# The first weight transfers and the last output tile of a hybrid attention layer: smaller loads, a warm-up from a constant, a residual added on TensorE, sums of squares from PSUM, and three last pieces stored from two queues

## The chip, the cores and the metric

The kernel runs on one core of one Trainium2 chip. The metric is the device time of one execution in microseconds, lower is better. The kernel before takes 434.15 us, the median of 3 runs (433.91 to 434.34).

## What is computed

One decoder layer over 512 tokens of width 1024, in float32. One wide input projection feeds two token mixers (a sparse attention with compressed, selected and window branches, and a gated linear recurrence); each mixer's result is gated and projected to 1024 channels, the two are merged by sigmoid gates, one output projection follows, and the layer ends in a residual with layer norm. The change touches the first product of the input projection and the last lines:

```
h = x @ w_in + b_in                       # first product here: the columns f_b of w_in
...
y = sigmoid(gm_a) * (o_a @ w_branch_a) + sigmoid(gm_b) * (o_b @ w_branch_b)
out = layer_norm(alpha * x + y @ w_out, ln_g, ln_b)
# layer_norm(v) = (v - mean(v)) * rsqrt(mean((v - mean(v))^2) + 1e-5) * g + b
```

## The kernel before, in words

Every float32 product is made of three float32r products: an operand is split into a high part (a cast) and a low part (what the cast left over), and `hi*hi`, `hi*lo` and `lo*hi` are added up in PSUM. A split takes one cast and one subtraction, mostly the cast on ScalarE (ACT) and the subtraction on VectorE (DVE).

**The head (lines 154 to 200).** x comes transposed, in 8 blocks of 128 channels by 512 tokens; the weights of the first product, `w0`, come in 8 blocks of 128 by 512 (64 KB per 128 columns). Block 0 of each is loaded in two halves of 256 columns: x from the SyncE queue (`dma`), the weights from the ACT queue (`dma_act`, line 158). The blocks 1 to 7 follow on the SyncE queue, x and weights in turn. While they travel, seven small matmuls of zeros run on TensorE (line 165), from a tile that DVE fills by a memset (line 162). Then, for block 0, ACT casts the x halves (`h`, line 183), DVE casts the weight halves (`wh`, line 184) and makes the two low parts (`l`, line 185, and `wl`, line 186); 24 matmuls of 256 columns use them, in the order (x half, weight half) = (0,0), (1,0), (0,1), (1,1). Each further block is split whole (lines 193 to 196) and feeds 12 matmuls of 512 columns.

**The middle.** Some 40 column tiles of the input projection are multiplied one after the other, and a table of delays weaves the steps of the two mixers between their matmuls. The branch products and the gates follow. The change leaves all this as it is.

**The end (lines 904 to 947).** `wo` holds the split halves of `w_out`, with the mean over the output channels taken out, so that `y @ wo` has mean zero over the channels; `res[tt]` holds `alpha * x`, mean taken out likewise, for token tile `tt` of 128 tokens, in two halves of 512 channels. For each token tile and half 24 matmuls add up in one PSUM bank. When they end, DVE adds half of the sum to the residual (line 933), collects `bn_stats` (line 934) and multiplies by `ln_g` (line 936). After both halves, `bn_aggr` (938) gives the variance, ACT takes the root (941), DVE its reciprocal (942), and DVE scales each half and adds `ln_b` (946); each half is stored by a DMA on the SyncE queue. The last token tile is cut in three in its matmuls (512, 256, 256 channels), with the multiplication of the last piece put behind the aggregate (944), but it is scaled and stored in two halves:

```
    cuts = [(0, 0, 512), (1, 0, 256), (1, 256, 512)] if last else [(0, 0, 512), (1, 0, 512)]
    ...
    if last:
        V.tensor_tensor(xr[hf][:, a:b], xr[hf][:, a:b], lg[hf][:, a:b], ALU.mult)
    for hf in range(2):
        V.scalar_tensor_tensor(xr[hf], xr[hf], rs[:, 0:1], lbn[hf], ALU.mult, ALU.add)
        dma(out[c, 512 * hf:512 * hf + 512], xr[hf])
```

**What sets the order.** Matmuls, DMAs and the marked DVE lines stay in program order; a scheduler places the rest on their engines and puts in the waits between engines. Each engine works through its own queue in order. A DMA takes one of eight landing semaphores in turn, and waits until the DMA eight places before it, on whichever queue, has landed.

Of the kernel before, what the change touches and what calls it, by code (L numbers as in the profile page):

```python
# [17 lines left out]
DM = 1024  # L18
P = 128
# [79 lines left out]
def layer_kernel(ctx: ExitStack, tc: tile.TileContext, xT, xn, w0, wi, wf, wv, small, brow, consts,  # L99
# [55 lines left out]
    halves = slice(0, 256), slice(256, 512)  # L155
    for n in halves:
        dma(first[0][:, n], xT[:, 0, n])
        dma_act(first[1][:, n], w0[0][:, n])
    act_set("sigmoid_and_others")

    zero = T2(128)
    V.memset(zero, 0.0)  # L162
# [7 lines left out]
    for kt in range(KT):  # L170
# [9 lines left out]
        if kt == 0:  # L180

            for n in halves:
# [731 lines left out]
    for tt in range(4):  # L914
        c = slice(128 * tt, 128 * tt + 128)
        last = tt == 3
        cuts = [(0, 0, 512), (1, 0, 256), (1, 256, 512)] if last else [(0, 0, 512), (1, 0, 512)]
        bst = SM(6 * len(cuts), "bst")
        xr = res[tt]
        bank = (PT, PO, PA, PS)[tt]  # L920
        pso_ = [bank() for _ in cuts[:2]] + ([PT()] if last else [])
        seq = [(u, kt) for u in range(len(cuts)) for kt in range(8)]
        if tt == 0:
            seq = [(u, kt) for kt in range(8) for u in range(2)]
        for u, kt in seq:
            hf, a, b = cuts[u]
            hi, lo = wo[kt][hf]
            ps = pso_[u][:, 0:b - a]
# [3 lines left out]
            if kt == 7:  # L932
                V.scalar_tensor_tensor(xr[hf][:, a:b], ps, 0.5, xr[hf][:, a:b], ALU.mult, ALU.add)  # L933
                V.bn_stats(bst[:, 6 * u:6 * u + 6], xr[hf][:, a:b])  # L934
                if not (last and u == 2):
                    V.tensor_tensor(xr[hf][:, a:b], xr[hf][:, a:b], lg[hf][:, a:b], ALU.mult)
        ag = SM(2, "ag")
        V.bn_aggr(ag, bst[:, 0:6 * len(cuts)])  # L938
# [4 lines left out]
        if last:  # L943
            V.tensor_tensor(xr[hf][:, a:b], xr[hf][:, a:b], lg[hf][:, a:b], ALU.mult)
        for hf in range(2):
            V.scalar_tensor_tensor(xr[hf], xr[hf], rs[:, 0:1], lbn[hf], ALU.mult, ALU.add)  # L946
            dma(out[c, 512 * hf:512 * hf + 512], xr[hf])
# [81 lines left out]
```

## Time and profile before

| | before |
|---|---|
| median of 3 runs | 434.15 us (433.91 to 434.34) |
| the profiled execution's own time | 433.26 us |
| its span, first to last instruction | 431.4 us |
| mean granted TensorE clock | 0.996 |
| busy: PE / weight loads / DVE / ACT / POOL | 98% / 82% / 69% / 57% / 4% |
| DMA, mean over the span | 110 GB/s |

The profile is of one execution. Its own time is 1.86 us over its span; that part lies outside the instructions. PE is TensorE's matmuls, PEld its weight loads, SPq and ACTq are the queues from which DMAs are issued. Matmuls overlap in the records, so that the pace of a row of them is read from the chain of waits and not from the duration of one. Times in the rows below are from the span's start.

### The profile page before, as it was taken

How to read it: one execution, taken by the hardware profiler on the slowest of the kernel's cores; microseconds unless marked ns; L12 is line 12 of the kernel's file. 1: busy time of each engine (PE TensorE's matmuls, PEld its weight loads, DVE VectorE, ACT ScalarE, POOL GpSimd, SP SyncE). 2: the span in 40 equal slices, each digit the busy share in tenths (PEclk: the TensorE clock that was granted, in tenths of full speed). 3: DMA queues.
4: the chain of work that ended last, by engine and by line, in shares of the span. 5: the costliest groups of instructions: out<-in, count | busy, mean ns of one | idle time of the engine just before them, and what ended most of it. 6: DMA issues, size and time to landing. Idle time of an engine off the chain costs nothing.

```text
span 431.4 us, 6047 instructions
## 1 busy us (share of the span) xinstructions
PE 424.1 (98%) x2173; PEld 355.3 (82%) x2173; DVE 298.6 (69%) x610; ACT 244.6 (57%) x490; POOL 16.0 (4%) x26
## 2 busy tenths in 40 slices
PE   9999999999999999999999999999999999999994
PEld 8888888888898878878888888888888888888884
DVE  5925669987786477956765666678655797872674
ACT  3434624713548455668866667788865975538300
POOL 2000000000011320000000010001001100000000
PEclk9999999999999999999999999999999999999998
DMA  8996400352320654141112111111144651072031
GB/s 271 394 356 217 148 1 2 85 149 87 123 73 2 188 147 152 52 145 50 49 51 95 49 51 49 50 49 55 45 148 160 215 161 50 0 217 77 19 129 49
DMA packets 20878, 47.57 MB, mean 110 GB/s; under 512 B 2928, under 2 KB 4592, under 8 KB 20848
## 3 DMA queue, kind: packets, MB, share of 16 engines
q1 hardware_dynamic: 20560, 46.92, 33.0%
q8 instruction: 17, 0.28, 0.3%
q10 hardware_dynamic: 288, 0.26, 0.2%
q14 instruction: 13, 0.11, 0.1%
HBM read 41.93 MB, written 2.10 MB: 102 GB/s over the span
## 4 chain that ended last, share of the span: by engine, by line
PE 98%; DVE 1%; DVEq 0%; issue 0%; ACT 0%
PE pa L107 62%; PE pss L107 17%; PE pso L107 12%; PE pst L111 5%; PE pst L107 3%; DVE t L946 0%; DVEq L1025 0%; DVE sm_bst L934 0%; DVE t L933 0%; ACT sm_rs L941 0%; DVE sm_ag L938 0%; DVE sm_rs L942 0%; DVE t L162 0%
## 5 line engine op out<-in xcount | busy, mean ns | idle before, releaser
L107 PE MATMUL pa<-t,whi 128*128 128x512 f32 x640 | 201.9, 397 | 0.0
L107 PEld LDWEIGHTS pa<-t,whi 128*128 128x128 f32 x640 | 116.9, 188 | 25.1 <-issue 2.0
L107 PE MATMUL pa<-t,wlo 128*128 128x512 f32 x320 | 125.2, 391 | 0.0
L151 DVE TENSOR_TENSOR wlo<-wraw,whi 128x1024 fp32r<-128x1024 f32 x46 | 57.0, 1241 | 23.4 <-ACT whi L150 23.1
L107 PEld LDWEIGHTS pa<-t,wlo 128*128 128x128 f32 x320 | 60.1, 188 | 13.2
L150 ACT CAST whi<-wraw 128x1024 fp32r<-128x1024 f32 x46 | 48.2, 1048 | 36.4 <-PE pa L107 17.7
L647 DVE CUSTOM_DVE_ANT_0 t<-pss,t 128x512 f32<-128x512 f32 (+3 forms) x64 | 30.1, 488 | 22.7 <-PE pss L107 22.5
L650 ACT ACTIVATE t<-t,sm_mn 128x512 f32<-128x512 f32 (+3 forms) x64 | 35.8, 561 | 9.0 <-DVE sm_mn L647 6.9
L151 DVE TENSOR_TENSOR t<-pst,t 128x512 fp32r<-128x512 f32 x40 | 27.5, 690 | 15.8 <-ACT t L150 15.8
L107 PE MATMUL pa<-t,t 128*128 128x512 f32 (+1 forms) x168 | 36.7, 375 | 0.0
L107 PEld LDWEIGHTS pa<-t,t 128*128 128x128 f32 x168 | 30.3, 188 | 5.6
L107 PE MATMUL pss<-t,t 128*128 128x512 f32 (+3 forms) x222 | 34.5, 310 | 0.0
L150 ACT CAST t<-pst 128x512 fp32r<-128x512 f32 x40 | 23.2, 580 | 18.9 <-PE pst L111 18.8
L107 PE MATMUL pso<-t,t 128*128 128x512 f32 (+2 forms) x158 | 32.9, 343 | 0.0
L107 PEld LDWEIGHTS pss<-t,t 128*128 128x128 f32 (+1 forms) x222 | 27.5, 175 | 3.7 <-issue 0.7
L111 PE MATMUL pst<-con,t 128*128 128x128 f32 x189 | 28.6, 272 | 0.0
L107 PEld LDWEIGHTS pso<-t,t 128*128 128x128 f32 x158 | 25.3, 190 | 3.8
L111 PEld LDWEIGHTS pst<-con,t 128*128 128x128 f32 x189 | 23.2, 140 | 4.2 <-DVE t L151 0.2
L107 PE MATMUL pso<-t,vv 128*128 128x512 f32 x80 | 23.1, 410 | 0.0
L151 DVE TENSOR_TENSOR t<-t,t 128x512 fp32r<-128x512 f32 (+1 forms) x22 | 14.2, 665 | 10.9 <-ACT t L150 10.9
L150 ACT CAST t<-t 128x512 fp32r<-128x512 f32 (+1 forms) x22 | 12.7, 603 | 15.5 <-DVE t L895 14.8
L107 PE MATMUL pss<-t,whi 128*128 128x512 f32 x64 | 19.7, 389 | 0.0
(166 smaller groups left out, 532.5 us busy)
## 6 DMA issues: line engine op xcount, KB each, us to landing
wraw<-in_wf_dram SPq DMA_DIRECT2D x38, 512.0 KB, 3.6
wraw<-in_wbr_dram SPq DMA_DIRECT2D x8, 512.0 KB, 3.8
t<-in_wout_dram SPq DMA_DIRECT2D x16, 256.0 KB, 3.2
t<-in_w_dram SPq DMA_DIRECT2D x15, 256.0 KB, 5.1
t<-t SPq DMA_DIRECT2D x48, 64.0 KB, 2.0
t<-in_wi_dram SPq DMA_DIRECT2D x8, 256.0 KB, 6.0
t<-in_xn_dram SPq DMA_DIRECT2D x8, 256.0 KB, 6.1
out_dram<-t SPq DMA_DIRECT2D x8, 256.0 KB, 2.1
```

The source lines that it names most:

```text
L107: return tc.keep_in_program_order(nc.tensor.matmul(*a, **k))
L111: return tc.keep_in_program_order(nc.tensor.transpose(*a, **k))
L150: A.copy(dst_hi, src)
L151: V.tensor_tensor(dst_lo, src, dst_hi.bitcast(F32), ALU.subtract)
L647: V.tensor_tensor_reduce(out=p[:, c], in0=ps[:, c], in1=amask[:, 512 - n:512], op0=ALU.add, op1=ALU.min, scale=-0.125, scalar=3.0e38, accu ...
L650: A.activation(p[:, c], p[:, c], AF.Exp, bias=mn[:, k], scale=-1.0, accum_out=den[:, k])
```

## The change

In the head, block 0's weights are loaded in three transfers of 128, 128 and 256 columns in place of two of 256, and cast in those pieces; the zeros of the warm-up are a constant that POOL writes in the program's preamble, and the memset on DVE goes.

In the last token tile the three pieces are written out by themselves. The first two are added to their residual on DVE as before, but ACT sums their squares (`Square` with an accumulator) in place of `bn_stats`; the mean is zero, so the mean square is the variance. For the third piece, twice the residual is split in high and low part ahead of time (`r2h`, `r2l`), and two matmuls with an identity (`eye`) add it in PSUM, after the first three matmuls of the piece. ACT then squares that piece from PSUM, takes the root of the total with what it knows of the first two pieces as the bias, DVE multiplies the piece by `ln_g` from PSUM, takes the reciprocal, and scales three pieces (512, 256, 256 channels), stored from the SyncE, ACT and SyncE queues.

```diff
+    wcuts = slice(0, 128), slice(128, 256), slice(256, 512)
     for n in halves:
         dma(first[0][:, n], xT[:, 0, n])
+    for n in wcuts:
         dma_act(first[1][:, n], w0[0][:, n])
...
-    zero = T2(128)
-    V.memset(zero, 0.0)
+    zero = nc.const_aps.tensor(0.0, [P, 128], F32)
...
             for n in halves:
                 A.copy(h[:, n], xr[:, n])
-                tc.keep_in_program_order(V.tensor_copy(wh[:, n], wr[:, n]))
-                tc.keep_in_program_order(V.tensor_tensor(l[:, n], xr[:, n], h[:, n].bitcast(F32), ALU.subtract))
-                tc.keep_in_program_order(V.tensor_tensor(wl[:, n], wr[:, n], wh[:, n].bitcast(F32), ALU.subtract))
+            for n, cuts in zip(halves, (wcuts[:2], wcuts[2:])):
+                for c in cuts:
+                    in_order(V.tensor_copy, wh[:, c], wr[:, c])
+                in_order(V.tensor_tensor, l[:, n], xr[:, n], h[:, n].bitcast(F32), ALU.subtract)
+                in_order(V.tensor_tensor, wl[:, n], wr[:, n], wh[:, n].bitcast(F32), ALU.subtract)
...
+    eye, r2h, r2l = T2(128, F32R), T2(256, F32R), T2(256, F32R)
+    rlast = res[3][1][:, 256:512]
+    V.tensor_copy(eye, ident)
+    A.activation(r2h, rlast, AF.Identity, scale=2.0)
+    V.scalar_tensor_tensor(r2l, rlast, 2.0, r2h.bitcast(F32), ALU.mult, ALU.subtract)
...
+    xr, ss, junk = res[3], SM(4, "ss"), T2()
+    for u, (hf, a, b) in enumerate(((0, 0, 512), (1, 0, 256))):
+        ps = PS()[:, 0:b - a]
+        for _ in outputs(ps, 3, hf, a, b):
+            pass
+        V.scalar_tensor_tensor(xr[hf][:, a:b], ps, 0.5, xr[hf][:, a:b], ALU.mult, ALU.add)
+        A.activation(junk[:, 0:b - a], xr[hf][:, a:b], AF.Square, accum_out=ss[:, u:u + 1])
+        V.tensor_tensor(xr[hf][:, a:b], xr[hf][:, a:b], lg[hf][:, a:b], ALU.mult)
+    V.tensor_scalar(ss[:, 0:1], ss[:, 0:1], 1.0 / DM, EPS, ALU.mult, ALU.add)
+    V.scalar_tensor_tensor(ss[:, 1:2], ss[:, 1:2], 1.0 / DM, ss[:, 0:1], ALU.mult, ALU.add)
+    ps = PT()[:, 0:256]
+    run = outputs(ps, 3, 1, 256, 512)
+    next(run)
+    T.matmul(ps, eye, r2h, start=False, stop=False)
+    T.matmul(ps, eye, r2l, start=False, stop=False)
+    for _ in run:
+        pass
+    with tc.issue_after(nat):
+        A.activation(junk[:, 0:256], ps, AF.Square, scale=0.5, accum_out=ss[:, 2:3])
+        A.activation(ss[:, 3:4], ss[:, 2:3], AF.Sqrt, scale=1.0 / DM, bias=ss[:, 1:2])
+    V.scalar_tensor_tensor(rlast, ps, 0.5, lg[1][:, 256:512], ALU.mult, ALU.mult)
+    V.reciprocal(ss[:, 3:4], ss[:, 3:4])
+    for hf, a, b, store in ((0, 0, 512, dma), (1, 0, 256, dma_act), (1, 256, 512, dma)):
+        V.scalar_tensor_tensor(xr[hf][:, a:b], xr[hf][:, a:b], ss[:, 3:4], lbn[hf][:, a:b], ALU.mult, ALU.add)
+        store(out[384:512, 512 * hf + a:512 * hf + b], xr[hf][:, a:b])
```

`outputs(ps, tt, hf, a, b)` is a generator that gives the 24 matmuls of one piece, three at a time. The token tiles 0 to 2 do what they did, in the same order.

Three places show what moved. In the rows a number behind a name tells buffers apart, and the bracket names the engines' and landing semaphores that the instruction waits for.

DVE, from the last piece's sum in PSUM to the end, before (t_3865 and t_3866 are the halves of the last token tile, t_3415 and t_3416 `ln_g`, t_3417 and t_3418 `ln_b`):

```order
L933 SCALAR_TENSOR_TENSOR t_3866<-pst,t_3866 128x256 [waits PE_49]
L934 BN_STATS sm_bst<-t_3866 128x6 [waits DVE_49]
L938 BN_AGGR sm_ag<-sm_bst 128x2 [waits DVE_49]
L944 TENSOR_TENSOR t_3866<-t_3866,t_3416 128x256
L942 RECIPROCAL sm_rs<-sm_rs 128x1 [waits Activation_49]
L946 SCALAR_TENSOR_TENSOR t_3865<-t_3865,sm_rs,t_3417 128x512 [waits DVE_49]
L946 SCALAR_TENSOR_TENSOR t_3866<-t_3866,sm_rs,t_3418 128x512
```

And now:

```order
L967 SCALAR_TENSOR_TENSOR t_3866<-pss,t_3866 128x256 [waits PE_49]
L969 TENSOR_TENSOR t_3866<-t_3866,t_3416 128x256 [waits Activation_49]
L971 SCALAR_TENSOR_TENSOR sm_ss<-sm_ss 128x1
L982 SCALAR_TENSOR_TENSOR t_3866<-pst,t_3416 128x256 [waits Activation_49]
L983 RECIPROCAL sm_ss<-sm_ss 128x1 [waits Activation_49]
L985 SCALAR_TENSOR_TENSOR t_3865<-t_3865,sm_ss,t_3417 128x512 [waits DVE_49]
L985 SCALAR_TENSOR_TENSOR t_3866<-t_3866,sm_ss,t_3418 128x256 x2
```

The residual's addition, `bn_stats` and `bn_aggr` of the last piece are gone; the product with `ln_g` (L982) reads PSUM and waits for ACT, namely for the square that reads the same bank; the last scaling is cut in two.

ACT at the end, now (before, its last work was the root L941 alone, four times, each waiting for DVE):

```order
L924 ACTIVATE t_3904<-t_3866 128x256 [waits Activation_49]
L955 ACTIVATE sm_rs<-sm_ag,epst 128x1 [waits DVE_49] x3
L968 ACTIVATE t_4108,sm_ss<-t_3865 128x512 [waits DVE_49,Activation_49]
L968 ACTIVATE t_4108,sm_ss<-t_3866 128x256 [waits DVE_49,Activation_49]
L980 ACTIVATE t_4108,sm_ss<-pst 128x256 [waits PE_49,Activation_49]
L981 ACTIVATE sm_ss<-sm_ss 128x1 [waits DVE_49,Activation_49]
L144 DMA out_dram<-t_3866 128x256 [waits DVE_49]
```

Three squares, the root behind the last of them, and one store stand there; `r2h` (L924) is made ahead of the roots of the first three token tiles.

DVE at the start, now (t_80 is block 0's weights, t_103 and t_104 their high and low part; t_79, t_101 and t_102 the same of x; before, a memset and one cast of 256 columns stood in place of the first two rows):

```order
L184 CAST t_103<-t_80 128x128 [waits DMAHW1_49]
L184 CAST t_103<-t_80 128x128 [waits DMAHW3_49]
L184 TENSOR_TENSOR t_102<-t_79,t_101 128x256 [waits DMAHW0_49,Activation_49]
L184 TENSOR_TENSOR t_104<-t_80,t_103 128x256 [waits DVE_49]
L184 CAST t_103<-t_80 128x256 [waits DMAHW4_49]
L184 TENSOR_TENSOR t_102<-t_79,t_101 128x256 [waits DMAHW2_49,Activation_49]
```

Both small casts stand ahead of x's low part, so that this now waits for the second small transfer too. Between the head and the end no engine's rows change their order, except for one cast (`eye`) and one subtraction (`r2l`) on DVE among the work of token tile 0.

## Rows read from the trace of the kernel before

**Rows 1.** The page's first lines: span, then busy us, share of the span and instructions by engine.

```profile
span 431.4 us, 6047 instructions
PE 424.1 (98%) x2173; PEld 355.3 (82%) x2173; DVE 298.6 (69%) x610; ACT 244.6 (57%) x490; POOL 16.0 (4%) x26
```

**Rows 2.** The chain of waits that ended last, its end in order of time: start us, us, what.

```profile
403.25 10.88 PE pa L107 x48
...
422.44 2.89 PE pst L107 x24
...
425.36 0.43 DVE t L933
...
425.82 0.44 DVE sm_bst L934
...
426.28 0.25 DVE sm_ag L938
...
426.55 0.30 ACT sm_rs L941
...
426.88 0.17 DVE sm_rs L942
...
427.07 0.75 DVE t L946
```

**Rows 3.** The timeline of the last microseconds, rows beside that chain: start us, us, engine, line, operation.

```profile
427.07 1.42 DVE L946 SCALAR_TENSOR_TENSOR t<-t,sm_rs,t 128x512 f32<-128x512 f32 x2
427.86 0.99 SPq L114 DMA_DIRECT2D out_dram<-t  x2
```

**Rows 4.** The last two stores by the tile view of the output, 427 us on: issue ns min/median/max with the first and the last start, and the time from issue to landing.

```profile
L114 SPq DMA_DIRECT2D out_dram<-t x2: 332/332/332, 427.9 to 428.5; - x2
...
DMA to landing us min/median/max: 2.0/2.0/2.1
```

**Rows 5.** Windows at the end: stretch, its us, busy us (x instructions) of PE, PEld, DVE, ACT, POOL, then the granted TensorE clock, the DMA engines' busy share, GB/s.

```profile
429.00:429.50 0.50, 0.00 (x0) 0.00 (x0) 0.00 (x0) 0.00 (x0) 0.00 (x0) 0.50 1.05 385
429.50:430.00 0.50, 0.00 (x0) 0.00 (x0) 0.00 (x0) 0.00 (x0) 0.00 (x0) 0.50 1.02 389
430.00:430.50 0.50, 0.00 (x0) 0.00 (x0) 0.00 (x0) 0.00 (x0) 0.00 (x0) 0.50 0.13 45
```

**Rows 6.** Groups of instructions by shape, over the whole span: line, engine, operation, out<-in, shapes, count, then busy us, mean ns of one, idle before.

```profile
L436 ACT COPY t<-pso 128x256 f32<-128x256 f32 x4 | 1.5, 368 | 0.0
L833 ACT ACTIVATION_READ_ACCUMULATOR t<-t 128x1 f32 x24 | 4.5, 187 | 0.0
L933 DVE SCALAR_TENSOR_TENSOR t<-pst,t 128x256 f32<-128x256 f32 x1 | 0.4, 424 | 1.5 <-PE pst L107 1.5
L663 DVE TENSOR_SCALAR t<-t,sm_dn 128x256 f32<-128x256 f32 x8 | 3.5, 490 | 0.1
```

**Rows 7.** The timeline of the end, where a sum over 512 columns is read out on ACT, and the last token tile's second piece on DVE.

```profile
400.01 0.61 ACT L833 ACTIVATE t<-t 128x512 f32<-128x512 f32 x1
400.53 0.19 ACT L833 ACTIVATION_READ_ACCUMULATOR t<-t 128x1 f32 x1
...
422.48 0.43 DVE L933 SCALAR_TENSOR_TENSOR t<-pss,t 128x256 f32<-128x256 f32 x1 [0.72 <-PE pss L107]
```

**Rows 8.** The timeline of the head, start us, us, engine, line, operation; in brackets the idle time before and what ended it.

```profile
0.73 0.90 ACTq L144 DMA_DIRECT2D t<-in_w_dram  x2
0.83 0.17 DVE L162 MEMSET t<- 128x128 f32 x1 [0.83 <-PEq L1017]
1.05 3.36 PE L107 MATMUL pso<-t 128*128 128x128 f32 x14 [1.05 <-DVE t L162]
3.65 0.40 ACT L183 CAST t<-t 128x256 fp32r<-128x256 f32 x1 [0.71 <-DMA t<-in_xT_dram]
3.85 0.30 DVE L184 CAST t<-t 128x256 fp32r<-128x256 f32 x1 [2.85 <-DMA t<-in_w_dram]
4.09 0.42 DVE L185 TENSOR_TENSOR t<-t,t 128x256 fp32r<-128x256 f32 x1
4.26 1.72 PEld L107 LDWEIGHTS pso<-t,t 128*128 128x128 f32 x12
4.97 0.42 DVE L185 TENSOR_TENSOR t<-t,t 128x256 fp32r<-128x256 f32 x1
6.91 0.43 DVE L194 CAST t<-t 128x512 fp32r<-128x512 f32 x1 [1.18 <-DMA t<-in_w_dram]
7.45 0.30 PEld L107 LDWEIGHTS pso<-t,t 128*128 128x128 f32 x2
8.45 0.42 DVE L194 CAST t<-t 128x512 fp32r<-128x512 f32 x1
```

**Rows 9.** DMA issues of the first 10 us: KB each, median us from issue to landing.

```profile
t<-in_w_dram ACTq DMA_DIRECT2D x2, 128.0 KB, 3.2
t<-in_xT_dram SPq DMA_DIRECT2D x2, 128.0 KB, 3.0
```

**Rows 10.** Windows in the head, columns as in rows 5. In the first both queues move data, in the second only SyncE's.

```profile
3.00:4.00 1.00, 1.00 (x7) 1.00 (x6) 0.15 (x1) 0.34 (x1) 0.00 (x0) 1.00 1.13 345
...
6.00:7.00 1.00, 1.00 (x11) 1.00 (x10) 0.10 (x1) 0.62 (x1) 0.00 (x0) 1.00 1.07 391
```

More of the change, by code (lines that the diff above doesn't have):

```diff
@@ L180, in layer_kernel, with in_order @@
         if kt == 0:
+            def in_order(op, *a):
+                tc.keep_in_program_order(op(*a))
             for n in halves:
                 A.copy(h[:, n], xr[:, n])
-                tc.keep_in_program_order(V.tensor_copy(wh[:, n], wr[:, n]))
-                tc.keep_in_program_order(V.tensor_tensor(l[:, n], xr[:, n], h[:, n].bitcast(F32), ALU.subtract))
-                tc.keep_in_program_order(V.tensor_tensor(wl[:, n], wr[:, n], wh[:, n].bitcast(F32), ALU.subtract))
+            for n, cuts in zip(halves, (wcuts[:2], wcuts[2:])):
[3 more added lines that the diff above has]
+                in_order(V.tensor_tensor, wl[:, n], wr[:, n], wh[:, n].bitcast(F32), ALU.subtract)
             for i, j in ((0, 0), (1, 0), (0, 1), (1, 1)):
@@ L913, in layer_kernel, with outputs @@
             A.activation(res[tt][hf], res[tt][hf], AF.Identity, bias=nm)
-    for tt in range(4):
-        c = slice(128 * tt, 128 * tt + 128)
[L916 to L926, printed above, removed]
+    eye, r2h, r2l = T2(128, F32R), T2(256, F32R), T2(256, F32R)
[3 more added lines that the diff above has]
+    V.scalar_tensor_tensor(r2l, rlast, 2.0, r2h.bitcast(F32), ALU.mult, ALU.subtract)
+    def outputs(ps, tt, hf, a, b):
+        c = slice(128 * tt, 128 * tt + 128)
+        for kt in range(8):
             hi, lo = wo[kt][hf]
-            ps = pso_[u][:, 0:b - a]
             T.matmul(ps, y[kt][0][:, c], hi[:, a:b], start=kt == 0, stop=False)
@@ L931, in layer_kernel @@
             T.matmul(ps, y[kt][1][:, c], hi[:, a:b], start=False, stop=kt == 7)
[L932 to L936, printed above, removed]
+            yield kt
+    for tt in range(3):
+        bst = SM(12, "bst")
+        xr = res[tt]
+        bank = (PT, PO, PA)[tt]
+        pso_ = bank(), bank()
+        runs = [outputs(pso_[hf], tt, hf, 0, 512) for hf in range(2)]
+        if tt == 0:
+            for _ in zip(*runs):
+                pass
+        for hf in range(2):
+            for _ in runs[hf]:
+                pass
+            V.scalar_tensor_tensor(xr[hf], pso_[hf], 0.5, xr[hf], ALU.mult, ALU.add)
+            V.bn_stats(bst[:, 6 * hf:6 * hf + 6], xr[hf])
+            V.tensor_tensor(xr[hf], xr[hf], lg[hf], ALU.mult)
         ag = SM(2, "ag")
-        V.bn_aggr(ag, bst[:, 0:6 * len(cuts)])
+        V.bn_aggr(ag, bst[:, 0:12])
         rs = SM(1, "rs")
@@ L942, in layer_kernel @@
         V.reciprocal(rs, rs)
-        if last:
-            V.tensor_tensor(xr[hf][:, a:b], xr[hf][:, a:b], lg[hf][:, a:b], ALU.mult)
         for hf in range(2):
             V.scalar_tensor_tensor(xr[hf], xr[hf], rs[:, 0:1], lbn[hf], ALU.mult, ALU.add)
-            dma(out[c, 512 * hf:512 * hf + 512], xr[hf])
+            dma(out[128 * tt:128 * tt + 128, 512 * hf:512 * hf + 512], xr[hf])
+    xr, ss, junk = res[3], SM(4, "ss"), T2()
+    for u, (hf, a, b) in enumerate(((0, 0, 512), (1, 0, 256))):
+        ps = PS()[:, 0:b - a]
+        for _ in outputs(ps, 3, hf, a, b):
+            pass
+        V.scalar_tensor_tensor(xr[hf][:, a:b], ps, 0.5, xr[hf][:, a:b], ALU.mult, ALU.add)
[9 more added lines that the diff above has]
+    for _ in run:
+        pass
+    with tc.issue_after(nat):
[6 more added lines that the diff above has]
+        store(out[384:512, 512 * hf + a:512 * hf + b], xr[hf][:, a:b])
 def _constants():
```

## The prediction

> **What bounds the kernel now.** I began with the page's first lines [rows 1]: TensorE is busy for 98% of the span, and no other engine for more than 82%. The reader should see that 424.1 of 431.4 us leaves 7.3 us in all, so that a change can gain only before TensorE starts, after it ends, or by taking matmuls away. The chain of waits [rows 2] shows the second place: the last 24 matmuls end at 425.33, and then six steps stand one behind another, none beside TensorE's work. The timeline [rows 3] adds the end of it: the two scalings run from 427.07 to 428.49 and the second store leaves at 428.52 (427.86 and 0.99, less its own issue of 0.33). By the tile view of the output [rows 4] it lands 2.0 us later, at about 430.5; the remaining 0.9 us to 431.4 is the program's closing, which I leave alone. The timeline of the head [rows 8] shows the first place: TensorE starts its zeros at 1.05, the first real weight load comes at 4.26, and the second block's at 7.45. So 5.2 us lie between TensorE's end and the last landing, and the head has its own chain. Everything between keeps its order and its matmuls.
>
> **The end, step by step.** Two matmuls of 256 columns are added. 24 of them take 2.89 us [rows 2], 0.12 us each, and TensorE has nothing to hide them: +0.24 us. The sum in PSUM is now complete at 425.57.
>
> Then ACT squares 256 columns from PSUM. No such square is in the trace. A copy of that shape from PSUM takes 0.37 us [rows 6]; a sum with an accumulator ends in a separate read of 0.19 us, which begins about 0.09 us before the main part ends (0.71 us for both over 512 columns) [rows 7]. That gives 0.47 us; I take 0.49, with 0.45 and 0.6 as ends (the second if an operand read per partition adds what it adds on DVE, some 0.07 us, and more). With 0.04 us of handing over, as between the steps of the old chain [rows 2], the square's result stands at 426.10.
>
> DVE's product with `ln_g` reads the same bank and waits for that square, so it doesn't run beside it: 426.13 to 426.55 at 0.42 us [rows 6]. Beside it ACT takes the root, 0.30 us as before [rows 2], done at 426.43. The reciprocal, behind the product on DVE, starts about 0.1 us before that one ends, as the scalings do: 1.42 us for two of 0.75 [rows 2, 3]. It ends at 426.63 and the first scaling starts at 426.67, against 427.07 before. What the old chain spent in residual sum, `bn_stats` and `bn_aggr` (0.43, 0.44, 0.25 us [rows 2]) has become a square, a product and two matmuls: of 0.4 us gained here, 0.24 us is already paid.
>
> The scalings are 512, 256 and 256 columns. The first follows the old pace of 0.67 us [rows 3]; one of 256 with an operand per partition takes 0.49 [rows 6], at a pace of some 0.40. So they end at 427.42, 427.83 and 428.23, and the last store leaves at 428.26, some 0.26 us before the old one.
>
> That store carries 128 KB where the old one carried 256. Both ends of its price: 2.0 us if size counts nothing [rows 4], and 1.66 if 128 KB less saves what 128 KB takes at 389 GB/s [rows 5], 0.34 us. I take neither: 512 KB leave within 0.8 us, the first from 427.45, whose packets should start 0.83 us later (the old first store left at 427.86 [rows 3]; the two together are 512 KB, and 385 to 389 GB/s until just after 430.0 [rows 5] puts their first packets at about 428.7). At 390 GB/s 512 KB need 1.34 us, to 429.62, and the landing at 430.5 follows the last packets, just after 430.0 [rows 5], by some 0.45 us. That gives 430.05, between 429.92 and 430.26. Against 430.5 the end gains **0.45 us**, with 0.15 and 0.65 as ends when the square's are added and times are rounded outward.
>
> Whether the second queue matters is part of that 430.05. In the head both queues load at once and move 345 GB/s together; SyncE's alone moves 391 [rows 10]. So I let the three stores share one stream. The Trainium skill's page "DMA: Bandwidth & Descriptors", section "Issuing engines are not separate DMA queues", says the same in stronger words: DMAs from all issuers run on the same 16 engines and interleave, and several issuers save only the time of issuing. By it 430.05 holds; were the queues independent, the last landing would be 429.92. And an issue takes 0.33 us [rows 4], less than the 0.40 us between two pieces, so there is nothing to save in issuing either.
>
> The same page, in "Anatomy of one DMA", puts a transfer at about 2.0 us fixed plus its bytes at 436 GB/s, a fit for another path. That is 2.6 us for 256 KB, where this trace has 2.0; taken at its word for 128 KB, 2.3 us, the last landing would be 430.56 and the end would gain nothing. The measurement decides; of the rule I keep the warning that most of a store's time does not shrink.
>
> The rest of the end lies under TensorE. The squares of the first two pieces replace their `bn_stats`; the second piece's chain on DVE begins at 422.48 with 0.43 us [rows 7], and square (0.49), product (0.42) and a sum of one column (about 0.2) bring it to 424.1, with 1.4 us before the last square needs it. Were that cover gone, the product L982 behind it would wait. `r2h` on ACT (0.4 us), `eye` (at most 0.3) and `r2l` (0.42) on DVE stand in token tile 0's work near 400 us, and delay its stores by under a microsecond; TensorE needs them at 422.8.
>
> **The head.** Three things move. The zeros need no memset, so TensorE can start when DVE did, at 0.83 in place of 1.05 [rows 8]: 0.22 us, and the zeros end so much earlier. The first real weight load waited for the weights' cast, which ended at 4.15; now the first small cast is early and it waits for x's cast, which ends at 4.05: 0.10 us. But neither reaches the second block. Its weights land at 6.9, their cast ends at 7.34, and TensorE loads them at 7.45 [rows 8]; TensorE would be ready at about 7.37, since the ninth of block 0's matmuls waits for x's second low part (done at 5.39) and sixteen at 0.12 us follow. So the most that block 0 can give is 0.08 us, and I count **0** for it. The other end is a loss: the second small transfer is issued one place later on ACT's queue (0.45 us, half of 0.90 [rows 8]), x's low part now stands behind its cast, and if it lands that much later, DVE's chain shifts by up to 0.4 us, of which 0.08 is hidden: 0.3 us lost.
>
> One transfer more also takes a landing semaphore more, so that SyncE's loads from the third weight block on wait for a landing one place earlier in the program. The cover is the third block: its weights' cast ends at 8.87 [rows 8], and TensorE comes to them twelve matmuls of 0.227 us (10.88/48 [rows 2]) after 7.45, at 10.2. 1.3 us of delay would cost nothing.
>
> **Sum.** 0.45 us at the end, 0 in the head. The profiled execution, 433.26 us, would become 432.81; the median of the runs shown, 434.15, lies 0.89 us above it, and the same 0.45 us off gives **433.7 us**. A measurement of this kernel can tell about 0.2%, 0.87 us, from no change; 0.45 us is inside that.
>
> **The rivals.**
>
> *The earlier start counts.* The runs' median is 0.89 us over the profiled execution, and no row says where. If the timed runs lose it in the head, with TensorE and not the second block's landing as the bound, then 0.22 us of earlier zeros counts in full, and 0.65 at the end makes 0.87 or a little more: 433.2 us. For it: the zeros run until 4.41, past the first real load [rows 8]. Against it: the second block's wait, and a clock that is granted in full, 2.4 GHz, wherever the head is read [rows 10]. The Trainium skill's "TensorE: Matmul & The Clock Gate", Part 1, has the clock low by default and raised by activity, so that an earlier start would also raise it earlier; by it the 0.22 us would bring up to 0.1 us more. The trace's windows don't bear it out.
>
> *ACT's store is the last to land.* On ACT's queue 128 KB took 3.2 us from issue to landing in the head [rows 9]. Its store leaves at 427.87; if it takes that long again, it lands at 431.07, 0.55 us after the old end: 434.7 us, slower than before. From 2.2 us on it is the last to land, from 2.65 on the kernel is slower. Against it: SyncE's 128 KB took 3.0 us there too [rows 9], where loads crowded one another, and 256 KB takes 2.0 at the end [rows 4].
>
> *The head pays.* The second small transfer, or the second block's weights, land 0.3 to 0.5 us later, and the end's gain is eaten: 434.1 us. Smaller packets and one place more on the queue speak for it, the 0.08 us of room against any cushion.
>
> **How the numbers follow.** The forecast has 0.60, the earlier start 0.17, ACT's store 0.10, the head's loss 0.13. The range is 433.15 to 434.45: the forecast's ends are 433.5 to 434.0 with 0.1 to 0.2 us for the runs' own spread (433.91 to 434.34), the lower end takes in the first rival, the upper one the third and half of ACT's. Faster by over 0.2% means under 433.28: most of the first rival and a corner of the forecast, 0.20. Slower by over 0.2% needs a loss of 0.87 us, a late ACT store and a late head together: 0.05. Within it: 0.75.
>
> **What would show it.** After the change the last matmul should end 0.24 us later in relation to the second block's first load; the square with its read should take 0.45 to 0.6 us; L982 should start only after it; the last store should leave about 2.7 us after the last matmul (3.2 before) and land under 2.0 us later. In the head, block 0's first load near 4.16, the second block's still near 7.45 behind its cast. I am wrong if that load moves by over 0.2 us either way, if ACT's store lands last, or if the store of 128 KB takes as long as one of 256.

## The result and the profile after

| | before | after |
|---|---|---|
| median | 434.25 us (6 runs, 433.44 to 435.15) | **438.31 us** (6 runs, 436.81 to 439.61) |
| ratio after / before | | **1.0092** (95% interval 1.0074 to 1.0109) |
| the profiled execution and its span | 433.26, 431.4 us | 438.75, 437.0 us |

4.06 us slower, where 0.45 us faster was forecast. The page's first lines after the change, to be read beside [rows 1]:

```profile
span 437.0 us, 6065 instructions
PE 427.6 (98%) x2175; PEld 357.4 (82%) x2175; DVE 297.9 (68%) x610; ACT 246.7 (56%) x497; POOL 15.9 (4%) x26
```

TensorE's share says nothing; the time left over does: 9.4 us where it was 7.3. The chain of waits of the changed kernel says where (start us, us, what):

```profile
1.67 6.36 DMA t<-in_w_dram
...
8.73 1.12 PE pso L107 x4
9.86 2.56 PE pss L107 x12
...
31.47 48.97 PE pa L107 x216
...
163.66 2.02 PE pss L107 x16
...
419.85 8.31 PE pss L107 x48
...
428.16 3.13 PE pst L107 x26
```

and the kernel before, at three of the same places:

```profile
6.19 1.43 PE pss L107 x12
...
26.77 48.96 PE pa L107 x216
...
158.96 1.02 PE pss L107 x16
```

The middle starts 4.70 us later (31.47 against 26.77), so most of the loss lies in the head. Another 1.0 us goes in 16 small matmuls near 160 us. From there to the last 48 + 24 matmuls nothing changes: 419.85 against 414.13 in [rows 2] is 5.72 us. The span grew by 5.6, so the end gave back 0.1.

**The head.** Its timeline after the change, beside [rows 8] (start us, us, engine, line, operation; in brackets the idle time before and what ended it):

```profile
3.90 0.29 PEld L107 LDWEIGHTS pso<-t,t 128*128 128x128 f32 x1
...
4.61 1.29 PEld L107 LDWEIGHTS pso<-t,t 128*128 128x128 f32 x7 [0.42 <-issue]
7.86 0.62 ACT L199 CAST t<-t 128x512 fp32r<-128x512 f32 x1 [3.38 <-DMA t<-in_xT_dram]
8.05 0.29 DVE L184 CAST t<-t 128x256 fp32r<-128x256 f32 x1 [2.89 <-DMA t<-in_w_dram]
8.26 0.75 DVE L184 TENSOR_TENSOR t<-t,t 128x256 fp32r<-128x256 f32 x2
8.73 0.83 PEld L107 LDWEIGHTS pso<-t,t 128*128 128x128 f32 x4 [2.84 <-DVE t L184]
12.01 0.44 PEld L107 LDWEIGHTS pso<-t,t 128*128 128x128 f32 x2
```

and its DMA issues of the first 10 us (KB each, median us to landing; [rows 9] before):

```profile
t<-in_w_dram ACTq DMA_DIRECT2D x2, 64.0 KB, 2.9
t<-in_w_dram ACTq DMA_DIRECT2D x1, 128.0 KB, 6.4
```

The first real load came earlier, as forecast (3.90; 4.26 before), and then after 8 of block 0's 24 matmuls TensorE stood still. The *third* weight transfer, the 256 columns that used to be second, took 6.4 us: it landed at 8.03, 0.19 us behind the second block's x, whose cast starts at 7.86 (6.25 before). DVE waited for it, and everything behind that wait with it. The second block's first load, which was to stay near 7.45, came at 12.01. A window (columns as in [rows 5]) shows what the idle time cost on top:

```profile
9.00:12.50 3.50, 3.50 (x18) 3.45 (x18) 3.50 (x9) 1.85 (x3) 0.00 (x0) 0.53 0.89 291
```

Behind the idle time the granted clock was at its lower level, 1.2 GHz: 0.53 here, and block 0's last 12 matmuls took 2.56 us where they had taken 1.43.

**The end** did nearly what was worked out:

```profile
431.38 0.38 ACT L980 ACTIVATE t<-pst 128x256 f32<-128x256 f32 x1 [2.15 <-PE pst L107]
431.66 0.19 ACT L980 ACTIVATION_READ_ACCUMULATOR t<-pst 128x1 f32 x1
...
431.88 0.42 DVE L982 SCALAR_TENSOR_TENSOR t<-pst,t 128x256 f32<-128x256 f32 x1 [2.13 <-ACT t L980]
...
432.41 1.54 DVE L985 SCALAR_TENSOR_TENSOR t<-t,sm_ss,t 128x512 f32<-128x512 f32 x3
433.19 1.16 SPq L114 DMA_DIRECT2D out_dram<-t  x2
433.59 0.35 ACTq L144 DMA_DIRECT2D out_dram<-t  x1
```

The last matmul ends at 431.29 (428.16 and 3.13), the last store leaves at 434.02: 2.7 us, as forecast. The stores of 128 KB took as long as one of 256, by the DMA issues of the end (KB each, us to landing):

```profile
out_dram<-t SPq DMA_DIRECT2D x3, 256.0 KB, 2.0
out_dram<-t ACTq DMA_DIRECT2D x1, 128.0 KB, 2.0
out_dram<-t SPq DMA_DIRECT2D x1, 128.0 KB, 2.0
```

### The profile page after: what moved, and what is told of

Same layout as the page of the kernel before. It is cut to its first block, busy times and chain, and to the rows that moved or that the text cites. A ratio compares the mean times of both kernels' runs of the same rounds, so it can differ in the third digit from the quotient of the medians.

```text
span 437.0 us, 6065 instructions
## 1 busy us (share of the span) xinstructions
PE 427.6 (98%) x2175; PEld 357.4 (82%) x2175; DVE 297.9 (68%) x610; ACT 246.7 (56%) x497; POOL 15.9 (4%) x26
## 4 chain that ended last, share of the span: by engine, by line
PE 97%; DMA 1%; DVE 0%; ACTq 0%; issue 0%; DVEq 0%; ACT 0%
PE pa L107 61%; PE pss L107 17%; PE pso L107 11%; PE pst L111 5%; PE pst L107 3%; DMA t<-in_w_dram 1%; DVE t L985 0%; ACTq L144 0%; DVE t L184 0%; DVE t L982 0%; DVEq L1064 0%; ACT t L980 0%; DVE sm_ss L983 0%; ACTq L980 0%
## 5 line engine op out<-in xcount | busy, mean ns | idle before, releaser
L107 PE MATMUL pso<-t,t 128*128 128x512 f32 (+2 forms) x158 | 34.1, 350 | 2.8 <-DVE t L184 2.8
L107 PE MATMUL pss<-t,t 128*128 128x512 f32 (+3 forms) x222 | 35.6, 317 | 0.0
L107 PEld LDWEIGHTS pss<-t,t 128*128 128x128 f32 (+1 forms) x222 | 28.7, 182 | 3.7 <-issue 0.7
```

The source lines that it names most:

```text
L107: return tc.keep_in_program_order(nc.tensor.matmul(*a, **k))
```

## The experiments

Theory: a transfer's landing is set by its place among the issues of both queues; the third weight transfer leaves beside the second block's x and lands with it. Rivals: the 512-byte packets of the small transfers slow all that follows; the constant or the new end costs the time; chance.

The kernel before ran beside each of them: its median was 434.26 us beside experiments 1, 2, 5 and 6, 434.41 beside 3, 4, 8 and 12, 434.25 beside 7, 10, 15 and 16, and 434.54 beside 9, 11, 13 and 14. Each ratio is to the kernel before, with its 95% interval; it is not exactly the quotient of the two medians, and where the two differ much both are given.

### Which part costs

**1. Halves again, in the transfers and in the casts, all else kept.**

```diff
-    wcuts = slice(0, 128), slice(128, 256), slice(256, 512)
+    wcuts = slice(0, 256), slice(256, 512)
```

> The changed kernel with block 0's weights in two transfers of 256 columns again; the constant for the warm-up and the new end stay. Place in the line (the third transfer lands behind SyncE's loads) and small packets both expect the whole loss gone and the end's gain left: about 433.8 us, 0.45 under before, second block's first load near 7.4 us. If the new end or the constant costs time, it stays above 435. If the 1 us lost again near 164 us in the changed kernel is not a child of the head's loss, it is here too: about 434.8.

Measured: 434.17 us, ratio to before 1.0006 (0.9995 to 1.0018). The loss is gone, so it is the three transfers'; the 0.45 us that the end was to leave as a gain doesn't show. The 1 us near 160 us was in this profile too, so it doesn't come from the head's loss.

**2. The three transfers alone**, with their casts, put into the kernel before.

```diff
+    wcuts = slice(0, 128), slice(128, 256), slice(256, 512)
...
+    for n in wcuts:
         dma_act(first[1][:, n], w0[0][:, n])
...
```

> The kernel before with the three transfers and their casts alone; memset and old end stay. Place in the line and small packets: all of the loss and none of the gain, 438.5 to 439, third transfer landing near 8 us, second block's first load near 12. If it is the constant or the end that costs: about 434.2.

Measured: 437.72, ratio 1.0079 (1.0062 to 1.0096). The third transfer landed at 7.45, x's cast began at 7.30, the second block's first load came at 11.31. Experiments 1 and 2 together place the loss.

**3. The constant alone** and **4. the new end alone**, in the kernel before.

```diff
-    zero = T2(128)
-    V.memset(zero, 0.0)
+    zero = nc.const_aps.tensor(0.0, [P, 128], F32)
```

> The kernel before with the warm-up's zeros from the constant, and nothing else. So far the second block's x landed at 6.06 to 7.84 us, in kernels with the constant (7.84, 7.32, 6.98, 6.06) and without it (6.23, 7.28). If that is chance, the constant is worth nothing in the timed runs: 434.1 to 434.3, since the second block waits for its loads. If TensorE's earlier start counts, 434.0; if the constant delays that load, x lands after 7 us and the time is 434.8 or more. The stall of 1 us in the 16 small matmuls near 160 us stood in every profile but the one of the kernel before: if its start is set by chance, it is as likely to be here as not, and is not due to this edit.

Measured: 434.49 beside 434.41, ratio 0.9996 (0.9986 to 1.0006): worth nothing that can be told. The second block's x was cast at 5.31 here, the earliest of all.

```diff
-    for tt in range(4):
+    eye, r2h, r2l = T2(128, F32R), T2(256, F32R), T2(256, F32R)
...
+        store(out[384:512, 512 * hf + a:512 * hf + b], xr[hf][:, a:b])
```

> The kernel before with the new end alone (residual on TensorE, squares, three pieces with stores on two queues). From last matmul to last landing the changed kernel took 4.70 us against 5.23 and its added matmuls took 0.24: the end by itself gains 0.2 to 0.3 us, 433.9 to 434.1. If it gains what was predicted, 433.8. If its work under TensorE (r2h, r2l, the squares) costs time in token tile 0 or 3, 434.4 or more, and TensorE's last 200 matmuls show a gap.

Measured: 433.96 beside 434.41, ratio 0.9990 (0.9980 to 1.0001). The sign and size of the forecast's end term, at the limit of what can be told.

### Place in the line, or small packets

**5. The third transfer from SyncE's queue, ahead of the second block's loads.**

```diff
-    for n in wcuts:
+    for n in wcuts[:2]:
         dma_act(first[1][:, n], w0[0][:, n])
+    dma(first[1][:, wcuts[2]], w0[0][:, wcuts[2]])
```

> The changed kernel with its third weight transfer issued from SyncE's queue, just ahead of the second block's loads, so that it leaves at the same 1.65 us but in front of them; the two small ones stay on ACT's queue. Place in the line: it lands near 4.7 us, the second block's loads 0.5 us later than before, first load near 7.9 and the kernel at 433.8 to 434.4. Small packets (the 512-byte packets of the first two slow what comes behind them): the third still lands after 6.5 us and the kernel stays above 436.5.

Measured: 436.62, ratio 1.0050 (1.0030 to 1.0069). The place theory's number was missed. The transfer landed at 5.96, before x (6.97) as it should, yet 1.3 us later than expected, and x itself 0.7 us later than in the kernel before. TensorE now waited only 0.19 us for the third transfer, but block 0's last 23 matmuls took 5.2 us (4.89 to 10.10), where experiment 14 below has 3.3. More than half of the loss stayed.

**6. Two halves, with 2 KB in between**, so that the second half leaves third, all in packets of 1 KB but for the 2 KB.

```diff
-    for n in wcuts:
-        dma_act(first[1][:, n], w0[0][:, n])
+    dma_act(first[1][:, wcuts[0]], w0[0][:, wcuts[0]])
+    dma_act(cst.tile([P, 4], F32, name="extra"), w0[0][:, 0:4])
+    dma_act(first[1][:, wcuts[1]], w0[0][:, wcuts[1]])
```

> The kernel of the first run of this set (two transfers of 256 columns) with a transfer of 4 columns (2 KB) between them on ACT's queue, so that the second half leaves one place later, near 1.65 us, with packets of 1 KB throughout. Place in the line: the second half lands near 8 us, TensorE idles some 2.8 us, 437 to 438.5 us. Small packets: it lands below 5 us and the kernel stays at 433.8 to 434.2.

Measured: 435.98 (435.16 to 438.45), ratio 1.0055 (1.0034 to 1.0075): 1.7 us lost by the medians, 2.4 by the ratio. That is neither theory's number; place had 437 to 438.5, packets 433.8 to 434.2. Its chain:

```profile
1.66 4.59 DMA t<-in_w_dram
...
6.96 0.74 PE pso L107 x4
7.70 1.43 PE pss L107 x12
```

The second half left at 1.66 and landed at 6.25, 0.19 us behind x, 1.8 us later than as second in the kernel before: the third place makes it late without small packets. x was early in this profile, so the wait was 1.23 us and the clock did not fall.

**7. The first two cut by partitions**, 64 rows of 256 columns each.

```diff
-    for n in wcuts:
-        dma_act(first[1][:, n], w0[0][:, n])
+    for p, n in ((slice(0, 64), halves[0]), (slice(64, 128), halves[0]), (slice(0, 128), halves[1])):
+        dma_act(first[1][p, n], w0[0][p, n])
```

> The changed kernel with three weight transfers as before it, but the first two cut by partitions (64 rows of 256 columns each) and not by columns: the same sizes at the same places in the queue, with packets of 1 KB where 512 bytes stood. Place in the line alone: as the changed kernel, 437.5 to 439, the second block's x lands at 7 to 8 us and the third transfer 0.2 us behind it. Small packets (in three profiles with them that x landed at 7.3 to 8.0, in seven without at 5.3 to 7.3): x lands below 6.6 us and the time is that of the run with an extra small transfer, 435.2 to 436.5.

Measured: 437.15, ratio 1.0082 (1.0064 to 1.0099). Inconclusive on the packets: the time is nearly that of the changed kernel with no 512-byte packet in it, but the second transfer of 64 rows landed only at 5.33 and TensorE began there (5.77), while x landed at 6.46. The time went another way than either theory had it.

**8. Two transfers, 128 and 384 columns**, the casts still in 128, 128 and 256.

```diff
+    wcuts = slice(0, 128), slice(128, 512)
```

> The changed kernel with block 0's weights in two transfers of 128 and 384 columns: the small first piece stays, with its 512-byte packets, and nothing is issued third. The casts stay 128, 128, 256. Place in the line: the second one leaves at 1.18 us beside x's second half and lands 0.2 us behind it, at 4.3 to 4.7, and the whole loss goes: 433.8 to 434.2. Small packets: half of the loss or more stays, 436 or more.

Measured: 434.92 (433.32 to 436.38), ratio 1.0012 (0.9998 to 1.0026). The small first piece with its 512-byte packets is here, and of the loss of 4 us only 0.5 is, within what can be told from nothing. So the packets alone are not the cause. Whether they add to the cost of the third place stays open: experiment 6 had the place without them and lost 1.7 to 2.4 us, not 4.

**9. A third transfer that nobody reads**, in the kernel before.

```diff
+    dma_act(cst.tile([P, 256], F32, name="extra"), w0[0][:, 0:256])
     act_set("sigmoid_and_others")
```

> The kernel before with a third transfer of 128 KB on ACT's queue that nobody reads. If a third transfer issued beside the second block's x delays that x by itself (7.05 us in the mean of seven profiles with one, 6.14 in six without): 0.5 to 0.9 us over before, 434.7 to 435.2, x at 6.5 to 7.5. If only its reader's wait counts: 434.3, x at 5.3 to 6.5.

Measured: 434.97 beside 434.54, ratio 1.0008 (0.9999 to 1.0017): 0.43 us, a little under the 0.5 expected, and its interval reaches down to nothing. x's cast began at 7.10. Over sixteen profiles (all but those of experiments 5 and 7) it began at 7.29 in the mean of nine in which ACT's third transfer left beside x (6.08 to 7.98), and at 6.16 in seven with two transfers on ACT's queue (5.31 to 7.34). So x does land later where a third transfer leaves beside it, 1.1 us in the mean; what that costs where nobody waits for the transfer itself is some 0.4 us, not clear of noise.

### What stands behind the wait, and the clock

**10. One DVE line moved**: the low part of x's second half, which needs no weights, ahead of the third piece's cast.

```diff
+                if n is halves[0]:
...
+                else:
+                    in_order(V.tensor_tensor, l[:, n], xr[:, n], h[:, n].bitcast(F32), ALU.subtract)
+                    for c in cuts:
+                        in_order(V.tensor_copy, wh[:, c], wr[:, c])
+                    in_order(V.tensor_tensor, wl[:, n], wr[:, n], wh[:, n].bitcast(F32), ALU.subtract)
```

> The changed kernel with one DVE line moved: the low part of x's second half, which needs no weights, stands ahead of the cast of the third piece and no longer behind it. If what is queued behind DVE's wait costs time: TensorE does four more matmuls before it waits (12 in place of 8) and starts again 0.4 us earlier after the third landing, so 0.7 to 1.3 us come back, 437.0 to 437.6. If only the landing counts: 438.3.

Measured: 435.88 (435.31 to 437.33), ratio 1.0054 (1.0033 to 1.0075). Against the changed kernel's 438.31 and 437.99 (experiment 11) that is 2.1 to 2.4 us back; by the ratios to the kernel before, 1.0092 and 1.0079, it is 1.1 to 1.7. So a third to somewhat over half of the loss hung on this line, as much as was expected or more. Its timeline:

```profile
4.57 2.39 PEld L107 LDWEIGHTS pso<-t,t 128*128 128x128 f32 x11 [0.39 <-issue]
...
7.62 0.29 DVE L184 CAST t<-t 128x256 fp32r<-128x256 f32 x1 [2.17 <-DMA t<-in_w_dram]
7.96 1.50 PEld L107 LDWEIGHTS pss<-t,t 128*128 128x128 f32 x12 [1.01 <-DVE t L184]
9.39 0.31 PEld L107 LDWEIGHTS pso<-t,t 128*128 128x128 f32 x2
```

The transfer was as late as ever (7.60). But 12 matmuls, not 8, came before the wait, TensorE idled for 1.01 us in place of 2.84, and it ran the second half at full speed.

**11. The changed kernel again**, beside experiments 9, 13 and 14 on one chip.

> The changed kernel once more. If its late landings and its fallen clock are its own: x of the second block at 7 to 8 us, third transfer 0.2 us behind it, clock down for some us behind TensorE's wait, 437.5 to 439. If they were chance: x near 6.2, 436 or less.

Measured: 437.99, ratio 1.0079 (1.0048 to 1.0110). Its chain:

```profile
1.66 5.34 DMA t<-in_w_dram
...
8.73 2.56 PE pss L107 x12
```

x a microsecond earlier than in the first profile (cast at 6.84), the rest the same: third transfer at 7.00, a wait of 2.19 us, 12 matmuls at half speed. The lateness and the fall are the kernel's own; how late x is varies.

**12. Five matmuls on zeros between the weight halves** and **13. six ahead of the wait.**

```diff
+            fill = PT()
...
+                for _ in range(5 if (i, j) == (0, 1) else 0):
+                    T.matmul(fill[:, 0:128], zero, zero, start=True, stop=True)
```

> The changed kernel with five more matmuls on zeros (2.1 us) between the two weight halves of block 0, so that TensorE is busy while it waits for the third transfer. Clock as a cost of its own: the second half's 12 matmuls run at full speed, 1.4 us in place of 2.6, and 0.9 to 1.2 us come back: 437.1 to 437.4. If the lower clock cost nothing (the second block would have waited for its loads anyway), 438.3, and the second block's first load is no earlier against the landing of the third transfer (4.0 us behind it in the changed kernel).

Measured: 440.11, ratio 1.0122 (1.0094 to 1.0149). Put in the wrong place: the wait is for x's low part, four matmuls before the second half, so that the zeros ran behind it (10.07 to 12.20) and only added their 2.1 us.

```diff
+            fill = PT()
...
+                    for _ in range(6 if (i, j) == (1, 0) and b is l else 0):
+                        T.matmul(fill[:, 0:128], zero, zero, start=True, stop=True)
```

> The changed kernel with six matmuls on zeros (1.3 us at full clock) ahead of the first matmuls that wait for x's second low part, so that TensorE's wait is half filled; an earlier run had such matmuls behind that wait, where they only added time. Clock as a cost of its own: no fall behind the wait, block 0's last 12 matmuls in 1.4 us in place of 2.6, 1 us back against the changed kernel beside it. If the fall costs nothing, or chance sets it, no difference.

Measured: 437.68 beside 437.99 for the changed kernel: no difference that can be told. The chain shows why, and something else:

```profile
5.16 1.89 PE pso L107 x7
7.05 2.56 PE pst L107 x12
9.61 0.61 PE pso L107 x4
10.22 1.43 PE pss L107 x12
```

The last 12 took 1.43 us as expected, but the six matmuls on zeros, twelve passes, ran at half speed and took 2.56 us in place of 1.3, past the landing at 7.83: what the clock gave back they had used. As a cost of its own the clock is not shown in times; only the profiles show it.

**14. Nine zeros in place of seven, on experiment 8's kernel.**

```diff
-    for _ in range(7):
+    for _ in range(9):
```

> The two-transfer kernel (128 and 384 columns) with nine matmuls on zeros in place of seven, which end at about 4.75 us, just before the second piece's matmuls can start (4.94 in its profile), so that TensorE has no pause of 0.5 us between its first and its third real load. In that profile the clock rose only at 9.8 us (4.5 to 5.5 in kernels without such a pause or with a short one), and block 0's second half went at half speed. If the pause keeps the clock low: 433.8 to 434.2 and the spread (433.32 to 436.38) gets narrow. If the rise is late by chance, the median stays at 434.9 with that spread.

Measured: 434.49 beside 434.54, ratio 1.0004 (0.9994 to 1.0014), spread 433.72 to 434.90. Experiment 8's chain first,

```profile
4.97 2.74 PE pso L107 x11
7.72 2.38 PE pss L107 x12
```

then this one's:

```profile
5.00 1.86 PE pso L107 x11
6.86 1.44 PE pss L107 x12
```

The same 23 matmuls took 5.1 and 3.3 us. The medians, each against its own base, differ by 0.5 us and their intervals overlap, but the spread is narrower: five of experiment 8's twelve runs took 435.36 to 436.38 us, more than any run of the kernel before beside them (at most 435.16), and here none took more than 434.90. That the pause behind the zeros was the reason is not shown, and this profile doesn't bear it out. The weight loads of the zeros, in experiment 8 and here:

```profile
0.74 3.06 PEld L107 LDWEIGHTS pso<-const-float32-0.0 128*128 128x128 f32 x14 [0.74 <-issue]
0.74 3.45 PEld L107 LDWEIGHTS pso<-const-float32-0.0 128*128 128x128 f32 x18 [0.74 <-issue]
```

The four added passes took 0.39 us, half of what four of the first fourteen take (0.87). So the clock was already up when they ran, before any pause, and it was the first fourteen, which experiment 8 has too, that preceded its rise. What brought it up so early here, and what narrowed the spread, stays open.

### The microsecond near 160 us, and a better kernel

**15. The new end, with the mixer's four products on DVE in place of POOL.**

```diff
-            G.tensor_tensor(o, o, rms[h], ALU.mult)
+            V.tensor_tensor(o, o, rms[h], ALU.mult)
```

> The kernel before with the new end alone, and the four products of the mixer's normalization on DVE in place of POOL. In eight of ten profiles one of POOL's products ran while DVE started a product or a weighted sum, which then took 1.78 to 1.87 us in place of 0.7, and TensorE stalled for 1 us in the 16 small matmuls near 160 us; in the profiles of the kernel before and of the new end alone it did not. If that collision costs most runs 1 us: 0.5 to 1 us under the new end alone (433.96), 433.0 to 433.4, and no stall in the profile. If DVE's four products of 0.7 us cost as much as they save, 434.

Measured: 433.72 (433.18 to 433.94), ratio 0.9989 (0.9977 to 1.0001). What it was to take away is seen in the timeline of the changed kernel,

```profile
160.70 1.32 POOL L472 TENSOR_TENSOR t<-t,t 128x512 f32<-128x512 f32 x1 [3.67 <-DMA t<-t]
160.79 1.78 DVE L576 TENSOR_TENSOR t<-t,t 128x512 f32<-128x512 f32 x1
162.60 1.26 ACT L579 CAST t<-t 64x512 fp32r<-64x512 f32 x2 [3.72 <-DVE t L576]
163.89 0.69 ACT L339 ACTIVATE t<-pa,sml 128x512 f32<-128x512 f32 x1
```

against the kernel before, where DVE happened to start first:

```profile
156.09 0.69 DVE L570 TENSOR_TENSOR t<-t,t 128x512 f32<-128x512 f32 x1
156.45 1.47 POOL L466 TENSOR_TENSOR t<-t,t 128x512 f32<-128x512 f32 x1 [4.66 <-DMA t<-t]
```

DVE's product took 1.78 us beside POOL's, ACT came late by as much, and four of the small matmuls waited for ACT's L339. Of 16 profiles with POOL's products 14 have this stall (1.96 to 2.05 us for the 16 matmuls); the first profile of the kernel before and that of experiment 4 do not. Without POOL's products they took 1.50, not 1.0: half of the stall went. The time, 0.53 us under its base where experiment 4 was 0.45 under its own, shows no further gain that can be told, and none of the 0.5 to 1 us expected.

**16. The same, with the second block's weights on ACT's queue as third transfer.**

```diff
+    second = T2()
+    dma_act(second, w0[1])
     act_set("sigmoid_and_others")
...
+        if kt > 1:
             dma(wr, w0[kt])
```

> The kernel of the run before this one in the set (new end, products on DVE) with the second block's weights issued from ACT's queue as its third transfer, beside that block's x on SyncE's. Pairing: they land 0.2 us behind x in place of 0.65, and the second block starts 0.3 to 0.5 us earlier wherever it waits: 432.6 to 433.0. If only the total of bytes counts, no change against that kernel.

Measured: 434.06, ratio 1.0004 (0.9991 to 1.0018). The second block's weights did land 0.19 us behind its x, but x's cast began at 7.36, so nothing was won. No kernel here beats the one before by more than can be told; experiment 15 is the nearest.

## Why the prediction was wrong

**The step that failed: the head counted as 0, 0.3 us at worst.** The prediction priced the *second* small transfer, which it saw issued one place later. The transfer that mattered, the third, with half of block 0's weights, it never priced. It had the view for it: in [rows 8] TensorE needs those weights (cast at 4.77, loads at 5.91) well before the second block's x lands, and the list of what is moved says that they now leave third. Three things followed.

- *It lands with x.* In nine profiles ACT's third transfer left within 0.03 us of SyncE's load of that x and landed 0.17 to 0.19 us behind it, at 6.2 to 8.1 us; as second it landed near 4.5. What the prediction quotes for the end from the Trainium skill's "DMA: Bandwidth & Descriptors", section "Issuing engines are not separate DMA queues", that DMAs from all issuers run on the same engines and interleave, should have been asked of the head: by it the third shares the stream with x's 256 KB, and these landings, under 0.2 us apart, agree. What its presence alone costs is about 0.4 us by experiment 9, somewhere between nothing and 0.7.
- *DVE's order.* The prediction saw x's first low part move behind the second small cast and named the queue, but not that the second low part stands behind the third cast. Four matmuls of x's second half, whose x and weights had long landed, waited for nothing else. Experiment 10 moved that one line, and was 1.6 us over its base by the medians (2.3 by the ratio), where the changed kernel was 3.5 (experiment 11) and 4.1 over theirs.
- *The clock.* From the third landing to the second block's first load 3.98 us went in the changed kernel (8.03 to 12.01) and 3.88 in experiment 11, 2.60 in experiment 6, where the same order stood but the wait was short and the clock stayed up, and 1.79 in experiment 10. So of the 2.1 us between experiments 10 and 11 there, some 0.8 is the line and 1.3 the clock that a shorter wait kept. That split rests on one profile each; no time shows it.

Against x's cast the second block's first load came 4.15 us later (7.86 to 12.01), against 1.20 before: 2.95 us, and x itself was 1.6 us later in the profile, by crowding and by chance.

**The clock was misread too.** The prediction took 1.00 in [rows 10] for a clock granted in full and set the first rival's rule aside with it. The pace says otherwise. Here is a window of experiment 13, columns as in [rows 5]:

```profile
7.00:9.00 2.00, 2.00 (x12) 2.00 (x11) 1.14 (x4) 0.63 (x2) 0.00 (x0) 1.00 1.05 390
```

It prints 1.00, and in it run the twelve passes of zeros over 128 columns that took 2.56 us, 0.21 each; the four such passes that experiment 14 added took 0.10 each. Experiment 8's 23 matmuls at 0.22 us stand under a printed 1.00 too, and twelve of the same shape took 0.12 each in experiment 13 (1.43 us). So early in these heads a printed 1.00 doesn't tell the two levels apart. The Trainium skill's "TensorE: Matmul & The Clock Gate", Part 1, has the clock low by default and raised by activity; the heads here agree, whose first zeros run at the slow pace (fourteen weight loads in 3.06 us in each of 17 profiles).

**The end: right in mechanism, its sum short of the forecast in the profile.** Two matmuls cost 0.24 us (3.13 against 2.89). Square and read took 0.47 (0.49 forecast), L982 waited for them, the last store left 2.7 us behind the last matmul (3.2 before). From there the term of the landing failed: 128 KB took 2.0 us from issue, like 256 KB; 1.8 was taken. From last matmul to the span's end 5.7 us went against 6.1, so the net gain was 0.1 in this profile. Over all profiles that stretch took 5.45 to 5.71 us (fourteen with the new end, 5.61 in the mean) and 5.99 to 6.07 (four with the old, 6.05): 0.44 us, of which the two matmuls take 0.24. So the end's term, 0.45, was about twice what the profiles give, 0.2. The 0.45 between the medians of experiment 4 equals the forecast, but its interval reaches from nothing to 0.9.

**Rivals.** *The head pays* had the sign and the place, with the wrong transfer and a tenth of the price. *ACT's store* landed in 2.0 us, not 3.2, before SyncE's last one. *The earlier start* alone (experiment 3) brought no earlier first load, 4.24 against 4.26, and no time. The prediction set it against a wait of the second block that [rows 8] doesn't show: the load at 7.45 stands without idle time before it. It was a near tie.

**The median over the profile**, 0.89 us that no row explained: the first profile of before is one of two without the stall near 160 us. That makes 1.0 of the 5.5 us between the two profiles, and chance of that size also lies in x's landing. In the medians it should be in both kernels; how often the timed runs have it stays open.

**The sum.** 2.95 us behind x and 0.4 of crowding, less 0.2 to 0.45 at the end, make 2.9 to 3.2 us; the medians differ by 4.06 and, in experiment 11, by 3.45. Several profiles together come closer than one pair. The second block's first load came at 12.01, 11.31 and 10.88 us in the changed kernel and experiments 2 and 11, 11.40 in the mean, and at 7.45, 8.50, 7.32, 7.96 and 7.62 in the kernel before and experiments 1, 3, 4 and 15, 7.77 in the mean. That is 3.6 us lost in the head, and 3.4 with the 0.2 gained at the end. What is left is of the size by which x's landing varies, and stays open.

## What to carry over

When a transfer is cut up, price the *last* piece, at the place in the common order of issue that it now has, and not the first piece that gets earlier. Follow from each wait what stands behind it on the same engine without needing it; moving such a line won back 1 to 2 us here, and the cut won nothing. A single profile's luck, a landing or a collision, can be as large as the effect that is to be read from it: look for the same row in several.

## What the hardware showed

- The second block's x was issued at 1.64 us in each of the 16 profiles of experiment 9, and its cast began between 5.31 and 7.98 us. Once the stream runs, a load of 256 KB lands about every 0.66 us (casts at 6.25 and 6.91 in [rows 8]).
- ACT's third transfer and SyncE's load of x, issued within 0.03 us, landed within 0.2 us of each other, nine times of nine.
- DVE's product of 128x512 took 0.69 us, and 1.78 where POOL's had started 0.09 us before it; POOL's took 1.47 where DVE's had started first, and 1.29 with DVE idle.
- At the end a store of 128 KB took 1.9 to 2.0 us from issue to landing and one of 256 KB 2.0 to 2.1, over 18 profiles.
- TensorE's clock first came up at very different times in the head: the last of 23 matmuls of block 0 ended at 8.3 us or at 10.1 in kernels that differ by two matmuls on zeros. What decides it is not shown.
